# Hybrid GDN block, opening rewritten: x turned before it is normalised, scaled by features on GpSimd; two column operations per block on ScalarE; the second half of x loaded already turned

## The chip, the cores and the metric

The kernel runs on one core of one Trainium2 chip. The metric is the device time of one execution in microseconds (us), the median of the runs. A profiled execution has its own time, and a span, which is the time from the first to the last recorded instruction.

## The reference

One residual block over x (1024 tokens by 1024 features, float32). Six rows of modulation come from a vector c; what the opening of the kernel computes is the first norm, its modulation and the projection of it:

```python
mod = (c_act @ w_ada[l] + b_ada[l])[:, None, :]
shift1, scale1, gate1, shift2, scale2, gate2 = jnp.split(mod, 6, axis=-1)
h = rms_norm(x, norm1_w[l]) * (1.0 + scale1) + shift1
x = x + gate1 * hybrid_mixer(h, w_in[l], ...)      # p = h @ w_in, then gated DeltaNet and a short conv
h = rms_norm(x, norm2_w[l]) * (1.0 + scale2) + shift2
x = x + gate2 * swiglu(h, w_gate[l], w_up[l], w_down[l])
return rms_norm(x, norm_f_w)
```

The norm divides each token (a row of x) by the root of its mean square, so its factor (called rs) belongs to a token; scale1 and shift1 belong to a feature.

## The kernel before, in words

The 1024 tokens are worked in two halves of 512. The 1024 features are eight blocks of 128 (k = 0 to 7). A matmul needs h by features: block k of h is a tile of 128 features by 512 tokens. Every float32 operand of the large products is split into a rounded part and a rest (both in the fast type fp32r, `h[:, 0]` and `h[:, 1]`, or `u[:, 0]` and `u[:, 1]`), and three products are added: high by high, low by high, high by low. TensorE is called PE below, VectorE DVE, ScalarE ACT, GpSimd POOL and SyncE SP.

The program has three orders. The first instructions, up to the accumulators `accs`, are written out by hand and kept in that order on each engine by `seq`. What follows, up to the second norm, is a set of tasks (`load0`, `sums0`, `xh0`, `wsplit0`, `acc0`, `h1_load`, `h1_work`, `fill`, and others). A planner (`Sim`) gives each operation a duration from `cost`, keeps a clock per engine that starts at `T_START`, and picks the next operation by time and the task's priority (`PR`); what it picks is the fixed order of each engine's queue. The rest is written by hand again. Every engine takes its queue strictly in order.

The opening, first half of the tokens:

- SP loads c, then four tiles of x of 128 tokens by 1024 features (`x0`), and then for each k 1 MB of `w_mod` (`wa`, the columns of scale1 and of shift1, turned) and 384 KB of `w_in0` (`wr`).
- `heat_up(n)` puts n matmuls of 128x128 on PE that compute nothing. `HEAT` holds how many at each place; in the trace each is two records. Two large matmuls (`c_ps`) spread silu(c) over the partitions, and DVE copies them into `c_bc`.
- For each tile of x, ACT takes the sum of squares (`norm_rs`), POOL turns it into rs (an add and a power), and DVE (tiles 0 and 1) or ACT (tiles 2 and 3) multiplies the tile by rs.
- `sums0`: for each k, DVE multiplies `wa` by `c_bc` and sums, twice; a small DVE operation after each makes the column `s1c[k]` (the factor of the feature) and `b1c[k]` (its offset).
- `xh0`: for each k, PE turns four 128x128 pieces of the scaled x into a PSUM bank (`tr`); `h_make` has ACT compute `h[:, 0]` and `hf` as tr times s1c plus b1c, and DVE subtract the two for the rest, `h[:, 1]`.
- `wsplit0`: for each k, ACT rounds `wr` into `whl[:, 0]` and DVE subtracts for `whl[:, 1]`.
- `acc0`: for each k, 18 matmuls (three products into six accumulators).

The second half of the tokens: `h1_load` loads four more tiles of x, computes rs for each and multiplies the tile by it on DVE; `h1_work` turns and modulates them in the same way as `xh0`, between the matmuls of `fill`, which multiplies all other columns of `w_in` (loaded as `raw`, split into `u`) by h into banks called `acc`.

Of the kernel before, what the change touches and what calls it, by code (L numbers as in the profile page):

```python
# [13 lines left out]
ALU = mybir.AluOpType  # L14
# [4 lines left out]
HEAT = (16, 2, 20)  # L19
# [15 lines left out]
T_START = (8.7, 10.2, 13.1, 11.7, 2.9)  # L35
# [16 lines left out]
def kernel(  # L52
    ctx: ExitStack,
    tc: tile.TileContext,
    x: bass.AP,
    c_cols: bass.AP,
# [170 lines left out]
    x0 = [xp.tile([P, D], F32, name=nm("x"), tag="x", bufs=8) for _ in range(4)]  # L227
# [18 lines left out]
    heat_up(HEAT[1])  # L246
# [7 lines left out]
    def norm_rs(t, pool, tag, jt="junk"):  # L254
# [4 lines left out]
        rs = pool.tile([P, 1], F32, name=nm("rs"), tag=tag + "r", bufs=4)  # L259
# [8 lines left out]
    late = []  # L268
    for i, t in enumerate(x0):
# [8 lines left out]
        if i == 1:  # L278
# [25 lines left out]
    class Sim:  # L304
# [68 lines left out]
        def cost(self, eng, op, a, k):  # L373
# [29 lines left out]
            elif eng == "pool":  # L403
                busy = 1.1 if op == "tensor_tensor" else 0.5
# [147 lines left out]
    for t, at in [(x0[0], 8.6), (x0[1], 10.0), (x0[2], 11.6), (x0[3], 13.1)] + [(cols_a, 5.0), (nb1, 10.2), (c_act, 4.0), (c_bc, 9.0)]:  # L552
# [7 lines left out]
    chb.take((3, 4, 5))  # L560
# [47 lines left out]

    def sums0():
        cb = c_bc.rearrange("p a b c -> p (a b c)")  # L610
        for k in range(KB):
            sim.wait(lambda: ("wa", k) in done)
# [11 lines left out]

    def xh0():
# [11 lines left out]
    def h_make(k, h, ps, first=None):  # L637
# [9 lines left out]
        free(ps)  # L647
# [3 lines left out]
    def wsplit0():  # L651
        for k in range(KB):
            sim.wait(lambda: k in wr)
# [3 lines left out]
            DVE.tensor_tensor(u[:, 1, :], wr[k], u[:, 0, :].bitcast(F32), ALU.subtract)  # L657
# [3 lines left out]
    def acc0():  # L661
        for _ in range(HEAT[2]):
# [129 lines left out]
    x1 = []  # L792
# [661 lines left out]
    for f, key in ((load0, "load0"), (sums0, "sums0"), (xh0, "h0"), (wsplit0, "w0"), (acc0, "acc")):  # L1454
        sim.spawn(f, PR[key])
# [673 lines left out]
def _laid_out(a):  # L2129
# [4 lines left out]
    d = {n: a[n] for n in ("x", "w_ada", "b_ada", "A_log", "dt_bias", "w_out", "w_gate", "w_up", "w_down", "norm_f_w")}  # L2134
    d["c_cols"] = col(a["c"])
# [10 lines left out]
_ARGS = ["x", "c_cols", "cols", "w_ada", "w_mod", "b_ada", "w_in0", "w_in", "w_ab", "A_log", "dt_bias", "w_out",  # L2146
# [37 lines left out]
```

## Time and profile before

| what | value |
|---|---|
| median of 3 runs | 1170.09 us (1170.09 to 1170.49) |
| profiled execution, its own time | 1170.96 us |
| span of the profiled execution | 1169.1 us |
| PE busy, matmul records | 1159.0 us (99%), 5586 |
| DVE, ACT, POOL busy | 922.0 us (79%), 539.5 us (46%), 61.2 us (5%) |
| mean granted TensorE clock | 0.999 |

In the rows of a timeline the first number is the start in us from the span's start, the second how long it lasted; then the engine (PEld is the weight load that goes ahead of each matmul), the line, the operation, what is written and read by the program's names, the shape, how many instructions were merged into the row (x12), and in brackets how long the engine had been idle and what released it. An instruction of DVE or ACT may start up to 0.1 us before the one ahead of it has ended, so how long a queue needs is read from start to start. Matmuls are pipelined and their ends are modelled, so PE too is read from start to start, on PEld.

### The profile page before, as it was taken

To read this page: it belongs to the slowest core of one execution; us is meant where nothing else is said; L and a number is where in the kernel's file an instruction comes from. 1 tells how busy PE (TensorE), PEld (TensorE's weight loads), DVE (VectorE), ACT (ScalarE), POOL (GpSimd) and SP (SyncE) were. 2 spreads that over 40 slices of the span, in tenths; PEclk is the share of its full clock that TensorE was granted. 3 is DMA by queue.
4 is the path that set the end of the run, shared out by engine and by line. 5 is a ranking of instruction groups with operands and counts; after the bars stand their busy time and mean duration, and the time that the engine had idled before them with its cause. 6 is when DMAs were issued, how large, how long until landed. Compare 5 with 4: busy or idle time off the path is not lost.

```text
span 1169.1 us, 16455 instructions
## 1 busy us (share of the span) xinstructions
PE 1159.0 (99%) x5586; PEld 969.4 (83%) x5586; DVE 922.0 (79%) x1718; ACT 539.5 (46%) x1168; POOL 61.2 (5%) x100
## 2 busy tenths in 40 slices
PE   9999999999999999999999999999999999999997
PEld 7888888888888988888888888888888888888886
DVE  7998988899977998668776777776777687788676
ACT  5688733469633643325433333333333365443343
POOL 2110101002000002100000000000000000000002
PEclk9999999999999999999999999999999999999999
DMA  9624365535215554434264456446554589869413
GB/s 360 257 64 146 106 186 158 174 116 161 81 57 163 164 187 153 194 97 139 95 214 151 149 199 225 151 139 221 192 182 135 197 303 391 310 203 339 146 36 144
DMA packets 126452, 207.06 MB, mean 177 GB/s; under 512 B 20512, under 2 KB 45088, under 8 KB 126368
## 3 DMA queue, kind: packets, MB, share of 16 engines
q1 hardware_dynamic: 120992, 202.80, 51.3%
q10 hardware_dynamic: 5376, 3.21, 0.9%
q8 instruction: 44, 0.72, 0.3%
q14 instruction: 40, 0.33, 0.1%
HBM read 150.91 MB, written 55.05 MB: 176 GB/s over the span
## 4 chain that ended last, share of the span: by engine, by line
PE 92%; DVE 4%; DMA 2%; ACT 1%; issue 1%; SPq 0%; POOL 0%; DVEq 0%; ACTq 0%; POOLq 0%
PE acc L88 34%; PE acc L450 24%; PE dn L88 17%; PE o L450 4%; PE o L88 4%; PE A L450 1%; PE K L450 1%; DVE xo L89 1%; PE ab L450 1%; PE tr L450 1%; PE w L450 1%; PE u L450 1%; PE qk L450 1%; PE kk L450 1%; DMA R<-in_w_gate_dram 1%
## 5 line engine op out<-in xcount | busy, mean ns | idle before, releaser
L450 PE MATMUL acc<-h,u 128*128 128x512 f32 x1200 | 300.2, 398 | 0.0
L450 PEld LDWEIGHTS acc<-h,u 128*128 128x128 f32 x1200 | 219.2, 188 | 41.6
L88 PE MATMUL acc<-h,hl 128*128 128x512 f32 x600 | 140.1, 390 | 0.0
L88 PEld LDWEIGHTS acc<-h,hl 128*128 128x128 f32 x600 | 112.4, 188 | 23.2
L88 PE MATMUL acc<-h,u 128*128 128x512 f32 x456 | 106.1, 389 | 0.0
L88 PE MATMUL acc<-T,hl 128*128 128x512 f32 x432 | 101.4, 390 | 0.1
L88 PEld LDWEIGHTS acc<-h,u 128*128 128x128 f32 x456 | 85.6, 188 | 17.8
L88 PEld LDWEIGHTS acc<-T,hl 128*128 128x128 f32 x432 | 80.9, 188 | 17.2 <-ACT cc L89 0.5
L88 PE MATMUL dn<-h,h 128*128 128x512 f32 x396 | 90.7, 389 | 0.0
L89 DVE TENSOR_TENSOR xo<-xo,dn 128x512 f32<-128x512 f32 x84 | 57.2, 686 | 42.0 <-PE dn L88 34.6
L89 ACT COPY cc<-acc 128x512 f32<-128x512 f32 x66 | 38.4, 590 | 108.3 <-PE acc L88 108.3
L88 PEld LDWEIGHTS dn<-h,h 128*128 128x128 f32 x396 | 74.3, 188 | 15.4
L88 PE MATMUL acc<-T,u 128*128 128x512 f32 x360 | 84.0, 389 | 0.0
L88 PEld LDWEIGHTS acc<-T,u 128*128 128x128 f32 x360 | 67.6, 188 | 14.0
L89 DVE TENSOR_TENSOR cc<-cc,acc 128x512 f32<-128x512 f32 x66 | 43.9, 684 | 29.8 <-PE acc L88 29.8
L450 DVE TENSOR_TENSOR u<-raw,u 128x512 fp32r<-128x512 f32 x82 | 56.3, 688 | 12.2 <-ACT u L450 12.0
L89 DVE TENSOR_TENSOR hl<-R,hl 128x512 fp32r<-128x512 f32 x60 | 39.5, 689 | 33.5 <-ACT hl L89 33.4
L450 ACT CAST u<-raw 128x512 fp32r<-128x512 f32 x61 | 37.8, 621 | 57.8 <-PE acc L450 52.9
L450 DVE SCALAR_TENSOR_TENSOR cv<-pr,cols_a,cv 128x512 f32<-128x512 f32 x72 | 53.2, 747 | 0.3 <-ACT cv L450 0.2
L89 ACT CAST h<-rw 128x512 fp32r<-128x512 f32 x57 | 32.7, 618 | 40.9 <-PE dn L88 34.6
L89 DVE TENSOR_TENSOR u<-R,u 128x512 fp32r<-128x512 f32 x46 | 30.1, 688 | 20.5 <-ACT u L89 20.5
L89 ACT CAST hl<-R 128x512 fp32r<-128x512 f32 x60 | 35.5, 622 | 23.1 <-DVE R L89 10.7
(339 smaller groups left out, 2002.0 us busy)
## 6 DMA issues: line engine op xcount, KB each, us to landing
raw<-in_w_in_dram SPq DMA_DIRECT2D x82, 256.0 KB, 3.1
am_scr<-cc SPq DMA_DIRECT2D x77, 256.0 KB, 4.5
raw<-in_w_ada_dram SPq DMA_DIRECT2D x56, 256.0 KB, 3.2
rw<-am_scr SPq DMA_DIRECT2D x55, 256.0 KB, 5.1
rw<-bm_scr SPq DMA_DIRECT2D x53, 256.0 KB, 5.3
bm_scr<-raw SPq DMA_DIRECT2D x51, 256.0 KB, 5.4
R<-in_w_gate_dram SPq DMA_DIRECT2D x22, 512.0 KB, 3.9
R<-in_w_up_dram SPq DMA_DIRECT2D x22, 512.0 KB, 5.3
```

The costliest lines, as they stand in the source:

```text
L88: return call(*a, **k)
L89: ins = call(*a, **k)
L450: ins = call(*a, **k)
```

## The change

The opening turns x as it comes, without its factor. PE transposes features 128 to 1023 of each tile (`xt`, seven pieces), and DVE (tiles 0 to 2) or ACT (tile 3) copies them into two new tiles `xT` of four feature blocks by 512 tokens. POOL writes a diagonal matrix of each tile's rs (`dgs`). A matmul of ones with it gives rs along the free axis, the same in every partition (`rs_ps`, copied to `RS0` by ACT), and a matmul of x's first 128 features with it gives block 0 turned and scaled at once (`x0_ps`). POOL then multiplies blocks 1 to 7 of `xT` by `RS0` (`x_last`), and `xh0` modulates them from there; the transpositions between the matmuls of `acc0` are gone. The two small operations after each sum are given to ACT. `HEAT` and the planner's start times are new, and three tasks get a priority that rises with k.

For the second half, the host lays x's second 512 tokens out by features as well (`x_t`), `h1_load` loads both layouts (the first only for the squares), spreads rs by one matmul into `RS`, and `h1_work` makes h from `x_t` with two DVE operations and one ACT operation per block and no transposition.

```diff
-HEAT = (16, 2, 20)
+HEAT = (6, 4, 6, 10, 6)
-T_START = (8.7, 10.2, 13.1, 11.7, 2.9)
+W_POOL = ()
+T_START = (11.9, 10.7, 10.0, 11.4, 2.9)
...
-    heat_up(HEAT[1])
...
-    def xnorm(t, pool):
-        rs = norm_rs(t, pool, "n1")[0]
-        DVE.tensor_scalar(t, t, rs, None, ALU.mult)
+    xT = [xp.tile([P, 4, HT], F32, name=nm("xT"), tag="xT", bufs=2) for _ in range(2)]
...
+    def x_part(i, b):
+        lo = 1 if b == 0 else 0
+        return xT[b][:, lo:4, i * P:(i + 1) * P], v3(xt_ps[i, b], 4)[:, lo:4, :]
+
+    heat_up(HEAT[1])
+    dgs = raw_t([P, 4, P])
     for i, t in enumerate(x0):
         rs, sq, p0, p1 = norm_rs(t, sp, "n1")
         seq("act", sq)
         seq("pool", p0)
         seq("pool", p1)
-        if i < 2:
-            seq("dve", DVE.tensor_scalar(t, t, rs, None, ALU.mult))
-        else:
-            late.append((t, rs))
+        seq("pool", POOL.tensor_scalar(dgs[:, i, :], ident, rs, None, ALU.mult))
+        for b in range(2):
+            ps = xt_ps[i, b] = xtb.get("xt")
+            for k in range(4 * b, 4 * b + 4):
+                if k:
+                    seq("pe", PE.transpose(ps[:, (k - 4 * b) * P:(k - 4 * b + 1) * P], t[:, k * P:(k + 1) * P], ident))
+            if i < 3:
+                seq("dve", DVE.tensor_copy(*x_part(i, b)))
+        heat_up(HEAT[2] if i < 3 else HEAT[3])
...
-    for t, rs in late:
-        seq("act", ACT.activation(t, t, AF.Copy, scale=rs))
+    x0_ps, rs_ps = misc.get(), misc.get()
+    for i, t in enumerate(x0):
+        seq("pe", PE.matmul(x0_ps[:, i * P:(i + 1) * P], t[:, 0:P], dgs[:, i, :], start=True, stop=True))
+        seq("pe", PE.matmul(rs_ps[:, i * P:(i + 1) * P], ones, dgs[:, i, :], start=True, stop=True))
...
                 if s_:
-                    DVE.scalar_tensor_tensor(s1c[:, k:k + 1], r, n1c[:, k:k + 1], nb1[:, k:k + 1], ALU.mult, ALU.add)
+                    ACT.activation(s1c[:, k:k + 1], r, AF.Identity, bias=nb1[:, k:k + 1], scale=n1c[:, k:k + 1])
                 else:
-                    DVE.tensor_tensor(b1c[:, k:k + 1], r, bac[:, k:k + 1], ALU.add)
+                    ACT.activation(b1c[:, k:k + 1], r, AF.Identity, bias=bac[:, k:k + 1])
...
+    def x_last():
+        for b in range(2):
+            ecopy(*x_part(3, b))
+        ecopy(RS0, rs_ps)
+        free(rs_ps)
+        for k in range(1, KB):
+            xk = xT[k // 4][:, k % 4]
+            POOL.tensor_tensor(xk, xk, RS0, ALU.mult)
+            done.add(("xn", k))
...
     def xh0():
         for k in range(KB):
-            ps = bank(chb, "tr")
-            for i in range(4):
-                tr(ps[:, i * P:(i + 1) * P], x0[i][:, k * P:(k + 1) * P])
-            sim.wait(lambda: ("cols", k) in done)
+            sim.wait(lambda: ("cols", k) in done and (k == 0 or ("xn", k) in done))
             h = h_slot(k, 0)
-            h_make(k, h, ps, h_hi)
+            h_make(k, h, xT[k // 4][:, k % 4] if k else x0_ps, h_hi)
...
     def acc0():
-        for _ in range(HEAT[2]):
+        for _ in range(HEAT[4]):
             mm(heat[:, 0:P], ones, ident)
...
     def h1_load():
         sim.wait(lambda: "loads0" in done)
-        for tt in range(4, 8):
-            x1.append(load_x(tt, xp, "x", 8))
-        for t in x1:
-            xnorm(t, sp)
+        for i in range(4):
+            t = load_x(4 + i, xp, "x", 4)
+            norm_rs(t, sp, "n1", rs=rs1[:, i:i + 1])
+        for j in range(2):
+            sim.wait(lambda: H[4 * j + 3][0] is not None)
+            t = xp.tile([P, 4, HT], F32, name=nm("xt"), tag="xT", bufs=2)
+            dma(t, x_t[4 * j:4 * j + 4].rearrange("k p c -> p k c"))
+            x1t.append(t)
+        dg = raw((P, 4, P))
+        DVE.tensor_tensor(dg, bc1(ident, 4), bc2(rs1, P), ALU.mult)
+        ps = bank(chb, "RS")
+        mm(ps, ones, flat(dg))
+        free(dg)
+        ecopy(RS, ps)
...
     def h1_work():
-            ps = bank(chb, "tr")
-            for i in range(4):
-                tr(ps[:, i * P:(i + 1) * P], x1[i][:, k * P:(k + 1) * P])
             h = h_slot(k, 1)
-            h_make(k, h, ps)
+            hf = hfs.tile(sp, [P, HT], F32, "hf")
+            DVE.scalar_tensor_tensor(hf, x1t[k // 4][:, k % 4], s1c[:, k:k + 1], RS, ALU.mult, ALU.mult)
+            ACT.activation(h[:, 0, :], hf, AF.Identity, bias=b1c[:, k:k + 1])
+            DVE.scalar_tensor_tensor(h[:, 1, :], hf, b1c[:, k:k + 1], h[:, 0, :].bitcast(F32), ALU.add, ALU.subtract)
```

In the rows of an instruction order that follow, a row is one instruction (or several alike, x3) with its line, operation, what it writes and reads, and the shape written. A name ends in the buffer's number: `x_100` to `x_103` are the four tiles of x, `ps_238` is x0_ps and `ps_239` rs_ps, `raw_138` is dgs, `xt_219` and `xt_223` are the two banks of tile 3.

The queue of PE from its first instruction to the first real matmul, before:

```order
L88 MATMUL heat<-ident,ones 128x128 x16
L88 MATMUL ps_130<-raw_128,ones 128x512
L88 MATMUL ps_134<-raw_132,ones 128x512
L88 MATMUL heat<-ident,ones 128x128 x2
L450 MATMUL heat<-ident,ones 128x128 x3
L450 MATMUL tr_192<-ident,x_100 128x128
L450 MATMUL heat<-ident,ones 128x128 x6
L450 MATMUL tr_192<-ident,x_101 128x128
L450 MATMUL heat<-ident,ones 128x128 x6
L450 MATMUL tr_192<-ident,x_102 128x128
L450 MATMUL heat<-ident,ones 128x128 x5
L450 MATMUL tr_192<-ident,x_103 128x128
```

The queue of PE in the same place, with the change, from the third tile of x on (ahead of these rows stand 6 heats, the two `c_ps`, 4 heats, and for each of the first two tiles 7 transpositions and 6 heats; behind them the two matmuls for each of the other three tiles and 6 more heats):

```order
L90 MATMUL xt_195<-ident,x_102 128x128 x3
L90 MATMUL xt_200<-ident,x_102 128x128 x4
L90 MATMUL heat<-ident,ones 128x128 x6
L90 MATMUL xt_219<-ident,x_103 128x128 x3
L90 MATMUL xt_223<-ident,x_103 128x128 x4
L90 MATMUL heat<-ident,ones 128x128 x10
L90 MATMUL ps_238<-raw_138,x_100 128x128
L90 MATMUL ps_239<-raw_138,ones 128x128
```

Twenty-eight transpositions, eight small matmuls and a different number of heats now stand ahead of the first real matmul, and the four transpositions of each block no longer stand among the real ones.

The queue of ACT between the squares of x's last tile and the first block of h, before:

```order
L89 ACTIVATE x_102<-x_102,rs_163 128x1024
L89 ACTIVATE x_103<-x_103,rs_169 128x1024
L450 CAST whl_198<-wr_195 128x768
L450 ACTIVATE h_0_37_240<-tr_192,b1c,s1c 128x512
L450 ACTIVATE hf_241<-tr_192,b1c,s1c 128x512
```

The same place of ACT with the change:

```order
L463 COPY xT_132<-xt_219 128x3x128
L463 COPY xT_133<-xt_223 128x4x128
L463 COPY RS_266<-ps_239 128x512
L463 ACTIVATE s1c<-mods,nb_130,cols_a 128x1
L463 CAST whl_275<-wr_272 128x768
L463 ACTIVATE b1c<-mods,cols_a 128x1
L463 ACTIVATE h_0_49_303<-ps_238,b1c,s1c 128x512
```

The copy of rs_ps, which needs PE's last small matmul, now stands ahead of the first block's columns, of its weight cast and of h.

The queue of DVE over one block of the opening, before:

```order
L450 TENSOR_TENSOR whl_244<-wr_201,whl_244 128x768
L450 TENSOR_TENSOR b1c<-mods,cols_a 128x1
L450 SCALAR_TENSOR_TENSOR wa_203,mods<-wa_203,c_bc 128x1024
L450 SCALAR_TENSOR_TENSOR s1c<-mods,cols_a,nb_142 128x1
L450 TENSOR_TENSOR h_0_44_278<-hf_279,h_0_44_278 128x512
L450 SCALAR_TENSOR_TENSOR wa_203,mods<-wa_203,c_bc 128x1024
```

DVE with the change, from the end of the hand-written part into the third block:

```order
L463 SCALAR_TENSOR_TENSOR wa_269,mods<-wa_269,c_bc 128x1024 x2
L463 TENSOR_TENSOR whl_275<-wr_272,whl_275 128x768
L463 SCALAR_TENSOR_TENSOR wa_274,mods<-wa_274,c_bc 128x1024
L463 TENSOR_TENSOR h_0_49_303<-hf_304,h_0_49_303 128x512
L463 SCALAR_TENSOR_TENSOR wa_274,mods<-wa_274,c_bc 128x1024
L463 TENSOR_TENSOR whl_307<-wr_278,whl_307 128x768
L463 SCALAR_TENSOR_TENSOR wa_280,mods<-wa_280,c_bc 128x1024
L463 TENSOR_TENSOR h_0_55_337<-hf_338,h_0_55_337 128x512
L463 SCALAR_TENSOR_TENSOR wa_280,mods<-wa_280,c_bc 128x1024
```

The two small operations per block have left DVE; what stays, two sums and two subtractions per block, reads two tiles each.

POOL with the change, from the last tile's rs on; before, its queue went from the power of tile 3 straight to the add of the second half:

```order
L91 TENSOR_SCALAR st_213<-st_213 128x1
L91 TENSOR_TENSOR rs_216<-st_213,nhalf 128x1
L91 TENSOR_SCALAR raw_138<-ident,rs_216 128x128
L463 TENSOR_TENSOR xT_132<-xT_132,RS_266 128x512 x3
L463 TENSOR_TENSOR xT_133<-xT_133,RS_266 128x512 x4
L463 TENSOR_SCALAR st_477<-st_477 128x1
```

Seven multiplications of 128x512 stand on POOL one behind the other, with nothing between them, where it had no work before.

More of the change, by code (lines that the diff above doesn't have):

```diff
@@ L55 @@
     x: bass.AP,
+    x_t: bass.AP,
     c_cols: bass.AP,
@@ L226 @@
     seq("sp", SP.dma_start(out=c_raw, in_=c_cols))
-    x0 = [xp.tile([P, D], F32, name=nm("x"), tag="x", bufs=8) for _ in range(4)]
+    x0 = [xp.tile([P, D], F32, name=nm("x"), tag="x", bufs=4) for _ in range(4)]
     for tt in range(4):
@@ L403, in cost @@
             elif eng == "pool":
-                busy = 1.1 if op == "tensor_tensor" else 0.5
+                busy = (1.1 if n < 128 else 0.1 + n * 0.0026) if op == "tensor_tensor" else 0.5
                 lat = busy + 0.15
@@ L551 @@
     sim.pipe = PIPE0
-    for t, at in [(x0[0], 8.6), (x0[1], 10.0), (x0[2], 11.6), (x0[3], 13.1)] + [(cols_a, 5.0), (nb1, 10.2), (c_act, 4.0), (c_bc, 9.0)]:
+    for t, at in [(t, 10.6) for t in xT] + [(xt_ps[3, 0], 10.0), (xt_ps[3, 1], 10.3), (x0_ps, 11.9), (rs_ps, 12.0), (cols_a, 5.0), (nb1, 9.7), (c_act, 4.0), (c_bc, 7.2)]:
         sim.acc[t.tensor.name] = [[0, P, 0, 1 << 30, at, True, None]]
@@ L559 @@
     dense.take((0, 1, 2))
-    chb.take((3, 4, 5))
+    chb.take((3, 4, 5, 6, 7))
     GP = {t: sim.res(t, 4) for t in ("at", "L", "WQ", "egl", "kt", "Tt", "bk", "nq", "bv")}
@@ L623, in sums0 @@
         done.add("ada0")
+    RS0 = sp.tile([P, HT], F32, name="RS0", tag="RS")
+    def x_last():
[7 more added lines that the diff above has]
+            done.add(("xn", k))
     def xh0():
         for k in range(KB):
[L627 to L630 removed]
+            at_k["h0"] = k
+            sim.wait(lambda: ("cols", k) in done and (k == 0 or ("xn", k) in done))
             h = h_slot(k, 0)
[L632 removed]
+            h_make(k, h, xT[k // 4][:, k % 4] if k else x0_ps, h_hi)
+            if not k:
+                free(x0_ps)
             H[k][0] = h
@@ L656, in wsplit0 @@
             w_hi[k] = u
-            DVE.tensor_tensor(u[:, 1, :], wr[k], u[:, 0, :].bitcast(F32), ALU.subtract)
+            (POOL if k in W_POOL else DVE).tensor_tensor(u[:, 1, :], wr[k], u[:, 0, :].bitcast(F32), ALU.subtract)
             free(wr[k])
@@ L1453 @@
     sim.spawn(h1_load, PR["h1"])
-    for f, key in ((load0, "load0"), (sums0, "sums0"), (xh0, "h0"), (wsplit0, "w0"), (acc0, "acc")):
-        sim.spawn(f, PR[key])
+    for f, key in ((load0, "load0"), (x_last, "setup"), (sums0, "sums0"), (xh0, "h0"), (wsplit0, "w0"), (acc0, "acc")):
+        sim.spawn(f, (lambda n=key: 0.3 + 0.01 * at_k[n] + PR[n] / 1000) if key in at_k else PR[key])
+    sim.own(x0_ps, chb, 6)
+    sim.own(rs_ps, chb, 7)
     for m in heads01:
```

22 lines of the change are left out of this document (15 added, 7 removed).

## The prediction

> **What bounds the kernel now.** The profile's page comes first: how busy each engine is, and the chain of work that ended last.
>
> ```profile
> PE 1159.0 (99%) x5586; PEld 969.4 (83%) x5586; DVE 922.0 (79%) x1718; ACT 539.5 (46%) x1168; POOL 61.2 (5%) x100
> PE 92%; DVE 4%; DMA 2%; ACT 1%; issue 1%; SPq 0%; POOL 0%; DVEq 0%; ACTq 0%; POOLq 0%
> ```
>
> PE is both the busiest engine and the chain. The waits of PE over the whole span have five groups; the two that the change can reach are
>
> ```profile
> PE acc L450 <- ACT h L450: 0.9, 1, 0.9
> PE tr L450 <- DVE x L89: 0.3, 1, 0.3
> ```
>
> So from the first real matmul on PE hardly ever waits. The time is then: when that matmul starts, plus all work queued on PE behind it, plus any wait that a change adds. I read each from the timeline of the opening, PE and its weight loads first:
>
> ```profile
> 1.44 5.33 PEld L88 LDWEIGHTS heat<-ident,ones 128*128 128x128 f32 x25 [1.44 <-POOL ident masks.py:199]
> 8.02 0.19 PEld L88 LDWEIGHTS ps<-raw,ones 128*128 128x128 f32 x1 [0.24 <-issue]
> 8.45 0.19 PEld L88 LDWEIGHTS ps<-raw,ones 128*128 128x128 f32 x1 [0.24 <-issue]
> 12.41 1.42 PEld L450 LDWEIGHTS heat<-ident,ones 128*128 128x128 f32 x12
> 13.75 0.14 PEld L450 LDWEIGHTS tr<-ident,x 128*128 128x128 f32 x1
> 13.86 1.20 PEld L450 LDWEIGHTS heat<-ident,ones 128*128 128x128 f32 x10
> 15.09 0.27 PE L450 MATMUL tr<-ident,x 128*128 128x128 f32 x1
> 15.40 0.78 ACT L450 ACTIVATE h<-tr,b1c,s1c 128x512 fp32r<-128x512 f32 x1 [1.53 <-PE tr L450]
> 16.23 0.96 PE L450 MATMUL acc<-h,whl 128*128 128x512 f32 x3 [0.87 <-ACT h L450]
> 25.40 0.60 PEld L450 LDWEIGHTS tr<-ident,x 128*128 128x128 f32 x4
> 25.97 4.05 PEld L450 LDWEIGHTS acc<-h,whl 128*128 128x128 f32 x18
> 30.06 0.59 PEld L450 LDWEIGHTS tr<-ident,x 128*128 128x128 f32 x4
> 52.88 3.63 PEld L450 LDWEIGHTS ab<-h,wab 128*128 128x128 f32 x16
> ```
>
> From these: warm, the 12 records of 6 heats take 13.75 − 12.41 = 1.34 us, 0.223 per heat; a transposition takes 13.86 − 13.75 = 0.11; a record of a large float32 matmul 8.45 − 8.02 = 0.43, two to a matmul. The first 25 heat records take about 0.213 each, twice the later rate, until about 6.7 us. One block of acc0 takes 30.06 − 25.97 = 4.09 for its 18 matmuls, and its four transpositions 25.97 − 25.40 = 0.57. The last transposition ended at 15.36, ACT began h at 15.40, and PE began 0.83 after that: 16.23. The eight blocks ended at 52.88.
>
> **Part 1, PE's queue ahead of the first matmul.** Now 6 heats at half speed, 12 × 0.213 = 2.56, end at 4.00. The two c_ps have four records, 0.85 each at half speed, 0.43 later; with the clock rising at 6.7 as before they end at 7.0. Then 4 heats, 28 transpositions, 28 heats and 8 small float32 matmuls of two records each (a heat's price): 0.89 + 3.1 + 6.25 + 1.8 = 12.0. PE queues these back to back, since x's tiles and rs come earlier: the last power on POOL ended at 11.94 before, and dgs adds one small operation.
>
> ```profile
> 10.97 0.97 POOL L89 TENSOR_TENSOR rs<-st,nhalf 128x1 f32<-128x1 f32 x1
> ```
>
> So rs_ps is there at 19.05 and a little, some 19.3. ACT's queue stands behind it, in the order shown: the copy of RS0, s1c, the weight cast, b1c, h. Their steps from start to start:
>
> ```profile
> 54.90 0.59 ACT L450 COPY pr<-acc 128x512 f32<-128x512 f32 x1 [1.64 <-DVE cv L450]
> 55.39 0.64 ACT L450 ACTIVATE qkT<-cv 128x512 f32<-128x512 f32 x1
> 44.93 0.84 ACT L450 CAST whl<-wr 128x768 fp32r<-128x768 f32 x1 [1.25 <-issue]
> 45.67 0.78 ACT L450 ACTIVATE h<-tr,b1c,s1c 128x512 fp32r<-128x512 f32 x1
> 2.57 0.21 ACT L89 ACTIVATE c_act<-raw 128x8 f32<-128x8 f32 x1
> ```
>
> Copy 0.5, cast 0.74, the two column operations 0.1 to 0.2 each (a tiny activation is 0.21 long): h begins at about 20.95, PE at 21.8, which is **+5.55** against 16.23. The six heats behind the small matmuls end before that. The clock's rise can shift this by about 0.9 either way.
>
> **Part 2, transpositions off PE's stream.** Seven groups stood between the blocks and eight in the second half: 15 × 0.56 = **−8.4**. The new matmul of RS has two records of 0.43: **+0.86**. Without any wait, parts 1 and 2 give −2.0.
>
> **Part 3, two column operations per block to ACT.** DVE's block before:
>
> ```profile
> 23.11 0.95 DVE L450 TENSOR_TENSOR whl<-wr,whl 128x768 fp32r<-128x768 f32 x1
> 23.98 0.15 DVE L450 TENSOR_TENSOR b1c<-mods,cols_a 128x1 f32<-128x1 f32 x1
> 24.05 1.22 DVE L450 SCALAR_TENSOR_TENSOR wa<-wa,c_bc 128x1024 f32<-128x1024 f32 x1
> 25.32 0.22 DVE L450 SCALAR_TENSOR_TENSOR s1c<-mods,cols_a,nb 128x1 f32<-128x1 f32 x1
> 25.72 0.69 DVE L450 TENSOR_TENSOR h<-hf,h 128x512 fp32r<-128x512 f32 x1 [0.18 <-ACT hf L450]
> 26.33 1.22 DVE L450 SCALAR_TENSOR_TENSOR wa<-wa,c_bc 128x1024 f32<-128x1024 f32 x1
> 27.47 0.95 DVE L450 TENSOR_TENSOR whl<-wr,whl 128x768 fp32r<-128x768 f32 x1
> ```
>
> 27.47 − 23.11 = 4.36 per block, under PE's 4.66. Without b1c and s1c and their waits it is 0.87 + 1.14 + 0.61 + 1.14 = 3.76, under PE's new 4.1 by only 0.34. So this part is worth nothing by itself and keeps DVE just ahead. ACT, with 0.4 more per block, has room. The loads are behind nothing new: their buffers (five of wa, three of wr) are freed by DVE, and they can run that many blocks ahead of it.
>
> **Part 4, seven multiplications on POOL.** The trace has none of 128x512. What it does have is POOL and DVE at once:
>
> ```profile
> 64.91 1.85 POOL L450 MEMSET xbd<- 128x1024 f32 x2 [4.15 <-DVE x L450]
> 66.02 0.76 DVE L450 TENSOR_SCALAR raw<-raw 128x16 f32<-128x16 f32 x1
> 376.25 1.63 POOL L450 COPY A<-xbd 32x256 f32<-32x256 f32 x3
> 376.80 0.83 DVE L450 TENSOR_TENSOR u<-raw,u 128x512 fp32r<-128x512 f32 x1 [1.53 <-ACT u L450]
> L450 DVE TENSOR_TENSOR u<-raw,u 128x512 fp32r<-128x512 f32 x82 | 56.3, 688 | 12.2 <-ACT u L450 12.0
> L450 POOL COPY A<-xbd 32x256 f32<-32x256 f32 x8 | 3.6, 455 | 7.8 <-DMA xbd<-dx 7.6
> ```
>
> DVE's tiny operation at 66.02 took 0.76 us and ended at 66.78, when POOL's second fill ended (64.91 + 1.85 = 66.76): held for the whole of POOL's instruction. The subtraction at 376.80 took 0.83 instead of the mean 0.688 beside POOL's copies. All four DVE operations of a block have that form, two tiles read from SBUF. So I expect POOL and DVE to take turns. [...]
>
> POOL's price p: its copy of 256 elements averages 0.455, so 512 elements with one input are about 0.8 to 0.9, and two inputs read in turn at most 1.8; below, DVE's own 0.69 is the least I allow. I take 1.2, nearer the copy's row. [...]
>
> Place: POOL begins when RS0 is copied, at 20.0. DVE waits for the first weight cast until 20.8, so one product is mostly covered. From then on they alternate until POOL is through: 7p + (0.87 + 1.14 + 0.61 + 1.14) × 2 = 7p + 7.52 after 20.0 the columns of block 2 are ready; column, h and the step to PE add 1.1. PE could have begun block 2 at 21.8 + 8.2 = 30.0. The loss is 7p − 1.4: **+7.0** for p = 1.2, 4.2 for 0.8, 11.2 for 1.8. After block 2 DVE needs 3.76 against 4.1 and PE does not wait again; the slack is too thin to give anything back, for PE cannot make up time. If POOL got in only where DVE idles, each block would pay about p less 0.34: 7 × 1.2 − 6 × 0.34 − 0.9 = 5.5.
>
> **Part 5, the second half.** DVE now does 16 operations of about 0.67 where it did 8 subtractions, four scalings of x and four of hf; some 1 us more, and 2 MB more are loaded. Both are spread over 40 us in which the matmuls of fill do not need h yet; I cost them at nothing. If that cover were gone, PE would wait about 1 to 3 us.
>
> **Sum.** 5.55 − 8.4 + 0.86 + 7.0 = +5.0. Against the profiled execution's own 1170.96 (span 1169.1) that is 1176.0; that execution lies 0.9 above the median of the runs, so I say 1175.1.
>
> **Rivals.**
>
> *POOL does not hold DVE.* For: a subtraction beside POOL lost only 0.14. Against: the row at 66.02. It would give −2.0, 1168.1. The point from which it decides: with p replaced by what DVE really loses per product, 7p − 1.4 is under 2.0 below 0.49 us, and the kernel is then not slower. Chance 0.22.
>
> *The heats cost less than their records.* If PE were through with its queue as soon as rs allows (12.2 + 1.8), RS0's copy starts at 14.3, h at 15.9, PE at 16.7 instead of 21.8: 5.1 less, 1170.0 with POOL's turns. For: the ends of matmuls are modelled, and nothing waits for a heat's result. Against: 0.223 per heat, measured with nothing else on PE. Chance 0.07.
>
> *PE's clock falls in the new waits.* PE would wait two or three times for about 2 us between 24 and 37 us. The first rows show heats at half speed until about 5 us of work had gone by; one such fall would cost 2.5 us or more: 1178 to 1181. Against: PE's longest wait in this trace after its start is the 0.9 us quoted above, so nothing shows a fall. [...] Chance 0.10.
>
> **How the numbers follow.** A measurement of this kernel can tell about 0.2%, 2.3 us. The forecast, 0.61, runs from 1172 to 1179 with p from 0.8 to 1.6 and the clock's 0.9, nearly all of it slower. The first rival lies 2.0 below, so split: 0.09 faster, 0.13 same; the second 0.06 and 0.01 for its two ends; the third slower. With 0.04 of the forecast within 0.2%: faster 0.15, same 0.18, slower 0.67. The range takes in the first rival below and most of the third above: 1167 to 1180.
>
> **What would show it.** Right: the first acc matmul near 21.8, after ACT's copy of RS0 near 19.3; POOL's products 1.0 to 1.6 us each, back to back or in turn with DVE; DVE's sums between 21 and 36 us starting late or lasting 1 us more than 1.22; PE waiting for ACT h in blocks 0 to 2 for some 7 us in all, and not afterwards; ab beginning near 61.7 instead of 52.88. Wrong: a first acc matmul before 18; DVE's steps at 3.8 per block beside POOL; a wait of PE after 65 us.

## The result: 0.5% slower, and the profile after

The changed kernel takes 1176.47 us (median, 1176.12 to 1177.55) beside 1170.34 us for the kernel before on the same chip: a ratio of 1.0049, with a 95% interval of 1.0039 to 1.006. The forecast was 1175.1 us, with a chance of 0.67 for slower by over 0.2%.

The busy times and the chain of the changed kernel's page:

```profile
PE 1161.2 (99%) x5580; PEld 969.6 (83%) x5580; DVE 925.1 (79%) x1702; ACT 541.7 (46%) x1186; POOL 72.9 (6%) x111
PE 90%; DVE 5%; ACT 3%; issue 1%; DMA 1%; POOL 0%; DVEq 0%; ACTq 0%; POOLq 0%
```

PE's share is 99% as before, and POOL, with 11.7 us more, goes from 5% to 6% and stays at 0% of the chain. Shares hide the loss. The waits of PE over the whole span (us in all, times, longest) show where to look:

```profile
PE acc L463 <- ACT h L463: 3.9, 3, 1.8
PE acc L463 <- DVE h L463: 1.0, 1, 1.0
```

Before, PE waited 0.9 us for h in all. The timeline of the opening has the cause (start, duration, engine, operation):

```profile
18.43 0.30 PEld L90 LDWEIGHTS ps<-raw,ones 128*128 128x128 f32 x2
18.96 0.58 ACT L463 COPY RS<-ps 128x512 f32<-128x512 f32 x1 [3.43 <-PE ps L90]
19.63 13.54 POOL L463 TENSOR_TENSOR xT<-xT,RS 128x512 f32<-128x512 f32 x7 [6.87 <-ACT RS L463]
20.78 0.78 ACT L463 ACTIVATE h<-ps,b1c,s1c 128x512 fp32r<-128x512 f32 x1
21.61 3.04 PE L463 MATMUL acc<-h,whl 128*128 128x512 f32 x12 [1.35 <-ACT h L463]
21.63 2.31 DVE L463 SCALAR_TENSOR_TENSOR wa<-wa,c_bc 128x1024 f32<-128x1024 f32 x1
23.88 1.76 DVE L463 TENSOR_TENSOR h<-hf,h 128x512 fp32r<-128x512 f32 x1
25.68 1.22 PEld L463 LDWEIGHTS acc<-h,whl 128*128 128x128 f32 x6 [1.46 <-DVE h L463]
27.79 2.01 DVE L463 TENSOR_TENSOR whl<-wr,whl 128x768 fp32r<-128x768 f32 x1
29.15 4.18 PEld L463 LDWEIGHTS acc<-h,whl 128*128 128x128 f32 x12 [2.25 <-ACT h L463]
...
33.64 1.21 DVE L463 SCALAR_TENSOR_TENSOR wa<-wa,c_bc 128x1024 f32<-128x1024 f32 x1
33.77 1.22 PEld L463 LDWEIGHTS acc<-h,whl 128*128 128x128 f32 x6 [0.44 <-DVE h L463]
34.78 0.95 DVE L463 TENSOR_TENSOR whl<-wr,whl 128x768 fp32r<-128x768 f32 x1
57.41 1.13 PEld L463 LDWEIGHTS ab<-h,wab 128*128 128x128 f32 x5
62.31 2.48 PEld L463 LDWEIGHTS ab<-h,wab 128*128 128x128 f32 x11
```

Three things are to be read here. PE's first real matmul starts at 21.61, 5.38 later than before. While POOL's seven products run, 19.63 to 33.17, every DVE operation but the first, six in all, lasts 1.06 to 1.10 us longer than later: a sum 2.31 instead of 1.21, the rest of whl 2.01 instead of 0.95, the rest of h 1.76 instead of the 0.69 of before. (The first, the rest of whl at 20.58, lasts 0.17 longer.) And five of ab's matmuls now stand inside acc0. Counted without them, acc0 ends at 62.31 − 1.13 = 61.18, where it ended at 52.88.

That moment splits the difference in two. Up to the end of acc0 the change loses 61.18 − 52.88 = 8.30 us; from there on it gains, since 1169.1 − 52.88 = 1116.2 us were left before and 1174.7 − 61.18 = 1113.5 now: 2.7. Together they are 5.6, the difference of the two spans. The same split is used for every experiment below ("up to acc0's end" and "rest"): acc0's end is the start of ab's last row less the time of ab's rows ahead of it.

### The profile page after: what moved, and what is told of

Same layout as the page of the kernel before. It is cut to its first block, busy times and chain, and to the rows that moved or that the text cites. A ratio compares the mean times of both kernels' runs of the same rounds, so it can differ in the third digit from the quotient of the medians.

```text
span 1174.7 us, 16452 instructions
## 1 busy us (share of the span) xinstructions
PE 1161.2 (99%) x5580; PEld 969.6 (83%) x5580; DVE 925.1 (79%) x1702; ACT 541.7 (46%) x1186; POOL 72.9 (6%) x111
## 4 chain that ended last, share of the span: by engine, by line
PE 90%; DVE 5%; ACT 3%; issue 1%; DMA 1%; POOL 0%; DVEq 0%; ACTq 0%; POOLq 0%
PE acc L90 35%; PE acc L463 22%; PE dn L90 17%; PE o L90 4%; PE o L463 4%; PE A L463 1%; PE heat L90 1%; PE K L463 1%; DMA raw<-in_w_ada_dram 1%; PE ab L463 1%; DVE xo L91 1%; DVE cv L463 1%; DVE u L463 1%; DVE T L91 1%; PE kk L463 0%
## 5 line engine op out<-in xcount | busy, mean ns | idle before, releaser
L463 ACT CAST u<-raw 128x512 fp32r<-128x512 f32 x65 | 40.2, 620 | 47.0 <-PE acc L463 44.7
```

The lines of the kernel that those rows point to most:

```text
L463: ins = call(*a, **k)
```

## The experiments

Ratios are to the kernel before, run alternately with each on the same chip, with 95% intervals; the changed kernel's is 1.0049. One per cent is 11.7 us.

| what | ratio | first acc | acc0's end | rest |
|---|---|---|---|---|
| before | 1 | 16.23 | 52.88 | 1116.2 |
| changed kernel | 1.0049 (1.0039 to 1.006) | 21.61 | 61.18 | 1113.5 |
| no products | 0.9995 (0.9986 to 1.0004) | 21.37 | 54.77 | 1113.2 |
| fills instead | 0.9995 (0.9986 to 1.0004) | 21.05 | 54.45 | 1113.8 |
| one-input products | 1.0003 (0.9994 to 1.0013) | 22.04 | 56.91 | 1114.2 |
| no heats | 1.0009 (1.0 to 1.0019) | 18.25 | 57.81 | 1112.4 |
| second half as before | 1.008 (1.0066 to 1.0094) | 22.38 | 62.12 | 1117.8 |
| second half alone | 1.0061 (1.0044 to 1.0078) | 16.21 | 59.78 | 1120.1 |
| columns on DVE | 1.0172 (1.0156 to 1.0187) | 21.41 | 64.56 | 1126.8 |
| columns on DVE, other order | 1.0067 (1.0053 to 1.008) | 21.82 | 65.15 | 1111.8 |
| changed, other order | 1.0128 (1.0114 to 1.0141) | 21.95 | 61.51 | 1125.2 |
| all turned by diag(rs) | 1.0037 (1.0023 to 1.005) | 16.89 | 51.35 | 1123.8 |
| the same, second order | 0.9975 (0.9966 to 0.9984) | 16.94 | 51.10 | 1117.2 |
| the same, third order | 0.9947 (0.9934 to 0.9961) | 17.17 | 51.05 | 1113.4 |

### Do POOL's products hold DVE?

```diff
-            POOL.tensor_tensor(xk, xk, RS0, ALU.mult)
```

> The changed kernel without GpSimd's seven multiplications of the turned x by RS; this leaves the factor rs out of blocks 1 to 7 of the first half. Turns theory (the 6.75 us that acc0 loses between its first matmul and its end come from VectorE and GpSimd taking turns): the loss goes, VectorE's sums last 1.22 us again from the start, TensorE still starts near 21.6, and the time is 1176.5 - 6.75 = about 1169.7 us. Rival (GpSimd does not hold VectorE; TensorE waits because the late start pushes ScalarE's and VectorE's work of the first blocks together): the waits of blocks 0 to 2 stay and the time stays at 1176 to 1177.

Measured: 0.9995, that is 0.54% or 6.3 us less than the changed kernel. The timeline of the opening without products, and its rows of ab:

```profile
21.22 1.22 DVE L463 SCALAR_TENSOR_TENSOR wa<-wa,c_bc 128x1024 f32<-128x1024 f32 x1
...
24.99 1.22 DVE L463 SCALAR_TENSOR_TENSOR wa<-wa,c_bc 128x1024 f32<-128x1024 f32 x1
28.75 1.22 DVE L463 SCALAR_TENSOR_TENSOR wa<-wa,c_bc 128x1024 f32<-128x1024 f32 x1
...
50.99 1.10 PEld L463 LDWEIGHTS ab<-h,wab 128*128 128x128 f32 x5
55.87 2.52 PEld L463 LDWEIGHTS ab<-h,wab 128*128 128x128 f32 x11
```

TensorE starts as late as in the changed kernel, but DVE's sums last 1.22 us from the first on, its block takes 28.75 − 24.99 = 3.76 us, and acc0 ends at 54.77, 6.4 earlier. PE then waits for nothing between its first acc and acc0's end. The late start alone doesn't make the waits. The turns do.

### Is it POOL's reading or POOL's being busy?

Two kernels put another POOL instruction in the same place, seven times, on RS's own tile.

```diff
-            POOL.tensor_tensor(xk, xk, RS0, ALU.mult)
+            POOL.memset(RS0, 0.0)                                # the first kernel
+            POOL.tensor_scalar(RS0, RS0, 1.0, None, ALU.mult)    # the second
```

> The changed kernel with each of GpSimd's seven multiplications replaced by a fill of RS's own 128x512 tile: GpSimd writes as much as before and reads nothing; this leaves the factor rs out of blocks 1 to 7 of the first half. If what holds VectorE is GpSimd's reading, its sums stay at 1.22 us beside the fills and the time is that of the kernel without products, 6 us under the changed kernel: a ratio to before of about 0.9995, 1169.7 us. If any GpSimd instruction takes its turn (a 128x1024 fill was 0.93 us in the trace of before, so half a microsecond for this one), seven turns cost about 3.5 - 1.4 = 2 us: 1171.8 us. If the length of the instruction does not matter, 1176.

> The changed kernel with each of GpSimd's seven multiplications replaced by a multiplication of RS's own 128x512 tile by 1.0: one input from SBUF in place of two; this leaves the factor rs out of blocks 1 to 7 of the first half. Theory (any GpSimd instruction that reads SBUF takes its turn, for as long as it lasts): a copy of 256 elements on 32 partitions was 0.455 us, so about 0.9 us each, a loss of 7 x 0.9 - 1.4 = 4.9 instead of 6.75: 1174.6 us, VectorE's sums 0.8 us longer than 1.22. Rival (only a GpSimd instruction with two inputs holds VectorE): like the run with fills, 1169.7 us, a ratio of 0.9995.

Measured: 0.9995 with fills, 1.0003 with one input. The timeline with fills, then with one input:

```profile
19.05 4.02 POOL L463 MEMSET RS<- 128x512 f32 x7 [6.11 <-ACT RS L463]
20.90 1.22 DVE L463 SCALAR_TENSOR_TENSOR wa<-wa,c_bc 128x1024 f32<-128x1024 f32 x1
```

```profile
20.06 13.98 POOL L463 TENSOR_SCALAR RS<-RS 128x512 f32<-128x512 f32 x7 [6.63 <-ACT RS L463]
21.89 1.63 DVE L463 SCALAR_TENSOR_TENSOR wa<-wa,c_bc 128x1024 f32<-128x1024 f32 x1
24.48 1.21 DVE L463 SCALAR_TENSOR_TENSOR wa<-wa,c_bc 128x1024 f32<-128x1024 f32 x1
25.63 1.35 DVE L463 TENSOR_TENSOR whl<-wr,whl 128x768 fp32r<-128x768 f32 x1
28.05 1.08 DVE L463 TENSOR_TENSOR h<-hf,h 128x512 fp32r<-128x512 f32 x1
```

Three operations of DVE fall beside the fills, and they last 0.96, 1.22 and 0.69 us, as without them: POOL's writing costs DVE nothing here. With one input POOL still needs 2.0 us per instruction from start to start, which fits waiting for DVE; but DVE loses only some 0.40 at a time, on each rest of whl or h (1.35 beside 0.95, 1.08 beside 0.69) and on the first sum (1.63), and nothing on the other sums. Against the run without products that is 56.91 − 54.77 − (22.04 − 21.37) = 1.5 us at acc0's end, or 0.9 in the median (the intervals overlap). Neither theory named this: it is a turn, but a shorter one, and why it spares the later sums is open. In these runs what held DVE was a POOL instruction that reads: 1.06 to 1.10 us at a time beside the products of two tiles, some 0.40 with one input, nothing beside the fills.

### Is the late start PE's own queue?

```diff
-HEAT = (6, 4, 6, 10, 6)
+HEAT = (6, 4, 0, 0, 0)
```

> The changed kernel with the 22 heats between the four transposed tiles and the 6 after RS left out (HEAT = (6, 4, 0, 0, 0)); nothing that is computed changes. Queue theory (the late start is TensorE's own queue ahead of RS): RS comes some 5.3 us earlier, TensorE starts near 16.3 instead of 21.6, and the time is 1176.5 - 5.3 = about 1171.2 us. Rival 1 (the start is set by the loads, the sums of squares and ScalarE's chain to rs): it starts no more than 2 us earlier, 1174.5 to 1176.5. Rival 2 (without heats the granted clock falls behind the gaps): transpositions and the first matmuls at half speed, 1176.5 or more.

The edit takes 28 heats out ahead of RS (three times six, and ten), not 22.

Measured: 1.0009, 4.7 us less than the changed kernel, near the 5.3 of the queue theory, but not by its way. PE starts at 18.25, not 16.3: the start gained 3.4, acc0's end 3.4 too, and 1.1 more of the span came later and is not assigned. The timeline shows what held the start:

```profile
12.03 1.21 DVE L463 SCALAR_TENSOR_TENSOR wa<-wa,c_bc 128x1024 f32<-128x1024 f32 x1
12.43 2.36 POOL L91 TENSOR_SCALAR raw<-ident,rs 128x128 f32<-128x128 f32 x1
13.17 1.21 DVE L463 SCALAR_TENSOR_TENSOR wa<-wa,c_bc 128x1024 f32<-128x1024 f32 x1
14.85 0.30 PEld L90 LDWEIGHTS ps<-raw,x 128*128 128x128 f32 x2 [2.27 <-POOL raw L91]
18.25 7.11 PE L463 MATMUL acc<-h,whl 128*128 128x512 f32 x18 [2.69 <-ACT h L463]
```

The last diag(rs), 0.62 to 0.64 us long for the other tiles, lasted 2.36. It started beside a sum of DVE and ended at 14.79, just behind the second sum (13.17 + 1.21 = 14.38). That fits the same turns with the roles changed, in this one case: DVE was first and POOL waited, and PE waited for POOL.

The rival on the clock was right in part. Behind idle weight loads of 2.27 and 2.88 us the first 18 matmuls took 7.11 us, beside 4.46 for a block in the trace of before, and the mean granted clock of the run was 0.996, beside 0.999. It doesn't show in the time: PE waited for h of block 1 behind them all the same (0.85 us), and block 1 began 3.4 us earlier than in the changed kernel, by as much as block 0 did.

### What are the transpositions of the second half worth?

One kernel takes the changed opening with the old second half, the other the old opening with the new second half.

```diff
-            t = load_x(4 + i, xp, "x", 4)              # changed kernel: also xT tiles, RS, no tr
+            x1.append(load_x(tt, xp, "x", 4))          # x by tokens, scaled on VectorE
...
+            ps = bank(chb, "tr")
+            for i in range(4):
+                tr(ps[:, i * P:(i + 1) * P], x1[i][:, k * P:(k + 1) * P])
```

> The changed kernel with the second half as it was: x by tokens, scaled on VectorE, eight groups of four transpositions, no RS matmul; the opening is the changed one. Theory (a group is worth its 0.56 us of TensorE wherever it stands): 1176.5 + 4.5 - 0.9 = about 1180 us, all of it after 61 us. Rival (the transpositions fill gaps, so the part by features brings nothing): 1176.5. Rival (the plan of the work that follows falls out otherwise, as in the kernel with the second half alone): a wait of several microseconds at a place that the edit does not touch.

Measured: 1.008, that is 0.31% or 3.6 us more than the changed kernel, as the theory had it. The size is in part luck: behind acc0 its PE has 2.3 us of small waits (K 1.0, A 0.9, G 0.4) that the changed kernel hasn't. In its timeline the transpositions stand in rows such as this one, 0.15 us each, between 76.4 and 88.5 us:

```profile
80.09 0.60 PEld L463 LDWEIGHTS tr<-ident,x 128*128 128x128 f32 x4
```

```diff
-    x0 = [xp.tile([P, D], F32, name=nm("x"), tag="x", bufs=8) for _ in range(4)]
+    x0 = [xp.tile([P, D], F32, name=nm("x"), tag="x", bufs=4) for _ in range(4)]
```

> The kernel before with the second half's part of the change alone: x of the second half loaded by features, no transpositions there, RS by one matmul; the opening is the old one. Theory (each group of four transpositions that leaves TensorE's queue is worth its 0.56 us, eight of them are 4.5, RS costs 0.86): 1170.3 - 3.6 = about 1166.7 us. Rival 1 (the transpositions lay in gaps of TensorE or VectorE's extra sum per block comes into the bound): 1170 to 1172. Rival 2 (loading x twice delays the second half's start by a wait): over 1172.

Measured: 1.0061, 11 us off the theory, and on the side of its second rival. This kernel doesn't test the transpositions, and the trace says why. Its longest wait of PE, and its timeline:

```profile
PE acc L452 <- ACT h L452: 5.5, 2, 4.6
```

```profile
43.73 0.49 PE L452 MATMUL tr<-ident,x 128*128 128x128 f32 x3
43.92 0.33 SPq L452 DMA_DIRECT2D x<-in_x_dram  x1
47.49 1.06 ACT L452 ACTIVATE jk<-x 128x1024 bf16<-128x1024 f32 x1 [5.13 <-DMA x<-in_x_dram]
52.65 0.76 ACT L452 ACTIVATE h<-tr,b1c,s1c 128x512 fp32r<-128x512 f32 x1
53.46 1.22 PE L452 MATMUL acc<-h,whl 128*128 128x512 f32 x2 [4.59 <-ACT h L452]
```

The tiles for the turned layout left room for four x tiles only, and the old opening reads its four until block 7 is turned (43.73). So the second half's first load is issued at 43.92, ACT's sum of squares stands in its queue waiting for it, and block 7's h stands behind that. acc0 ends 6.9 later. The new second half needs the new opening, which is through with x's tiles when its last small matmul has read them, at 18.7. The rest is 3.9 longer than before, too, where 3.6 less was expected; PE waits there for raw (1.9 us) and for A (1.6), in another order of the later work. How much of them the turned loads cause was not separated.

### Are the columns better on DVE?

```diff
-                    ACT.activation(s1c[:, k:k + 1], r, AF.Identity, bias=nb1[:, k:k + 1], scale=n1c[:, k:k + 1])
+                    DVE.scalar_tensor_tensor(s1c[:, k:k + 1], r, n1c[:, k:k + 1], nb1[:, k:k + 1], ALU.mult, ALU.add)
-                    ACT.activation(b1c[:, k:k + 1], r, AF.Identity, bias=bac[:, k:k + 1])
+                    DVE.tensor_tensor(b1c[:, k:k + 1], r, bac[:, k:k + 1], ALU.add)
...
-BIAS = dict(dve=0.3)     # the second kernel only
+BIAS = dict(dve=0.45)
```

> The changed kernel with its two column operations per block (s1c and b1c of the first half) back on VectorE. Turns theory: VectorE's block grows by two column operations, about 0.6 us, in the stretch in which GpSimd holds it back (blocks 0 to 2, some 2 us) and is about as long as TensorE's 4.1 afterwards: 1177.5 to 1179.5 us. Rival (the columns on ScalarE hold up h and cause part of TensorE's waits for ScalarE): 1 to 3 us faster than the changed kernel, 1173.5 to 1175.5.

> The changed kernel with the column operations of the first half back on VectorE, as in the run before of that kind, with one number of the planner changed (BIAS of VectorE 0.3 to 0.45) so that the order of the later work comes out anew. In the earlier run the stretch of 20 to 40 us lost 3.8 us more than in the changed kernel, and 10 us more were lost between 400 and 510 us. Theory (only the first is the price of the two operations): 1176.5 + 3.8 = about 1180 us, a ratio of 1.008. Rival (the columns on VectorE really cost 15 us): about 1191.

Measured: 1.0172 and 1.0067. The first is 12 us over the top of its forecast, nearly all of it in the rest; the second is near its 1.008. Up to acc0's end both lose about the same against the changed kernel, 3.4 and 4.0 us, where about 2 was expected at first. In the timeline of the second:

```profile
26.36 1.24 DVE L463 SCALAR_TENSOR_TENSOR s1c<-mods,cols_a,nb 128x1 f32<-128x1 f32 x1
30.60 1.21 DVE L463 TENSOR_TENSOR b1c<-mods,cols_a 128x1 f32<-128x1 f32 x1
31.73 1.21 DVE L463 SCALAR_TENSOR_TENSOR wa<-wa,c_bc 128x1024 f32<-128x1024 f32 x1
31.90 0.81 ACT L463 ACTIVATE h<-xT,b1c,s1c 128x512 fp32r<-128x512 f32 x1 [8.75 <-DVE b1c L463]
32.77 7.22 PEld L463 LDWEIGHTS acc<-h,whl 128*128 128x128 f32 x21 [5.04 <-ACT h L463]
36.65 0.15 DVE L463 TENSOR_TENSOR b1c<-mods,cols_a 128x1 f32<-128x1 f32 x1
```

An operation on one column, 0.15 us at 36.65, lasts 1.21 beside a product: it can pay a whole turn, however small. But the sum right behind it (31.73) pays none. The seven products hold DVE for 6.7 us in all, here as in the changed kernel: the price was the same with nine DVE operations beside the products as with seven there. What the columns cost is their place in the queue. Block 1's b1c now stands behind s1c and the rest of whl, which in the changed kernel are not ahead of it, so ACT's h starts at 31.90 instead of 28.29, PE waits 5.04 us for it, and block 1 begins at 32.77, where the changed kernel begins it at 29.15. That is 3.6 of the 4.0 us. Moving the two columns to ACT is worth that much beside the products; without products it was not tried. The first kernel's rest is 13.3 longer than the changed kernel's. About half of that is one wait of PE, for the split of the last gate's sum:

```profile
PE row L90 <- ACT Tt L463: 6.8, 1, 6.8
```

That wait is gone in the second kernel, whose later order was dealt anew by one number of the planner; its rest is even 1.7 shorter than the changed kernel's.

### A version without the products

If the loss is turns and a late start, both can go: turn and scale every block, not only block 0, by a matmul with diag(rs).

```diff
-                    seq("pe", PE.transpose(ps[:, (k - 4 * b) * P:(k - 4 * b + 1) * P], t[:, k * P:(k + 1) * P], ident))
+                seq("pe", PE.matmul(to, t[:, k * P:(k + 1) * P], dgs[:, i, :], start=True, stop=True))
...
-        ecopy(RS0, rs_ps)
-            POOL.tensor_tensor(xk, xk, RS0, ALU.mult)
```

> A version meant to beat both: the second half as in the changed kernel; in the first half all eight blocks, not only block 0, are turned and scaled in one matmul against diag(rs), so RS0, GpSimd's products and all heats after the first ten go, and the turned blocks are copied out of PSUM by VectorE (tiles 0 and 1) and by the planned copies (tiles 2 and 3). The small matmuls wait for diag(rs) of each tile. Theory: no turns, TensorE starts near 16.3 to 18.3 (GpSimd's last diag(rs) waited 2 us for VectorE in the run without heats), and the rest is the changed kernel's: 1176.5 - 6.75 - 3.3 to 5.3 = 1164.5 to 1166.5 us. Rival (the clock of TensorE stays low without the heats, or VectorE's copies hold up its sums): 1168 or more.

Measured: 1.0037, not the gain. The opening does what it should: the first acc at 16.89, acc0's end at 51.35, 9.8 before the changed kernel. The rest is 10 us longer. Its longest wait of PE, and the windows behind it (us, busy time of PE, PEld, DVE, ACT and POOL with counts, granted clock, DMA share, GB/s):

```profile
PE row L90 <- ACT Tt L460: 6.7, 1, 6.7
```

```profile
482.00:486.00 4.00, 3.65 (x8) 2.64 (x9) 1.00 (x2) 4.00 (x8) 1.43 (x5) 0.50 1.01 409
486.00:490.00 4.00, 4.00 (x14) 3.16 (x13) 1.37 (x2) 0.46 (x2) 1.67 (x4) 0.67 0.81 325
```

PE waits 6.7 us, then runs at half its clock (0.50), and still at 0.67 in the four microseconds after that. A new opening makes the planner deal out another order 400 us later, and in this order PE reaches the last gate's matmul before its sum is ready.

Two more orders of the same kernel, each by numbers of the planner alone:

```diff
-MARGIN = dict(pe=0.6)
+MARGIN = dict(pe=0.7)                            # second order
-BIAS = dict(dve=0.3)                             # third order, with MARGIN 0.7
+BIAS = dict(dve=0.25)
-T_START = (14.9, 11.6, 10.0, 12.8, 2.9)
+T_START = (14.2, 11.0, 10.0, 12.8, 2.9)
```

> The version with all eight blocks turned and scaled by diag(rs), with one number of the planner changed (MARGIN 0.6 to 0.7), so that it writes the order after 65 us out anew; in the first version TensorE waited 6.7 us at 475 us for the split of the last gate's sum, which stood too early in its queue, and ran at half speed for some us after it, 9 to 10 us in all. Theory (that wait is an accident of the order, not a price of the opening): it goes, and the time is 1175.9 - 9.4 = about 1166.5 us, a ratio of about 0.995. Rival (whatever the order, something the opening saved is paid back later): a wait of similar size elsewhere, 1174 or more.

> The version with all eight blocks turned and scaled by diag(rs), with the planner's numbers set otherwise again (MARGIN 0.7, BIAS of VectorE 0.25, TensorE's and VectorE's start times 14.2 and 11.0 instead of 14.9 and 11.6). The first order of this version gave 1175.9, the second 1168.0 us with some 7 us of small waits left between 20 and 400 us. Theory (the opening is worth about 10 us against the changed kernel, and an order decides how much of it is kept): no wait over 2 us after 65 us, 1164 to 1168 us. Rival (the gain of the second order was a lucky one): 1172 or more.

Measured: 0.9975 (1167.99 us) and 0.9947 (1166.08 us, beside 1171.58 for the kernel before in the same comparison). In the second the wait is gone, but its rest is still 3.8 us longer than the third's, in smaller waits, so the theory's 1166.5 was missed by 1.5. Both orders beat the kernel before and the changed one, the third by 0.5% and 1.0%. Its longest wait of PE, but for the first heat's:

```profile
PE acc L460 <- ACT h L460: 1.5, 1, 1.5
```

Was it the planner's number rather than the opening? The changed kernel with that number alone:

> The changed kernel, nothing edited but the planner's MARGIN, 0.6 to 0.7, as in the second order of the turned and scaled version. It separates the planner's number from the opening. Theory (the number only deals the later order out anew; here the planner's own account puts VectorE's last work 22 us behind TensorE's instead of 9, as in the first order of the turned and scaled version): the opening loses the same 6.75 us, a wait for the split of the last gate's sum of some 7 us comes up near 475 us, 1185 us. Rival (MARGIN 0.7 is the better number for any opening): under 1174.

Measured: 1.0128, 9 us worse than the changed kernel. Up to acc0's end nothing moved (61.51), and the wait came up where it was looked for:

```profile
PE row L90 <- ACT Tt L463: 7.7, 1, 7.7
```

So the number is not better in itself; it deals another order, good for one opening and bad for another. What all three orders of the new opening share is acc0's end, 51.05 to 51.35, some 10 us before the changed kernel's. How much of that reaches the end depends on the order: three were tried for this opening, two for the changed kernel and one for the kernel before, so the 0.5% is the opening together with a chosen order.

## Why the prediction was right, point by point

**Part 1, the late start.** Predicted +5.55, measured +5.38. The last small matmul's weights were loaded by 18.73 where 19.05 was worked out, ACT's steps came in the listed order (copy at 18.96, h at 20.78), and the first acc at 21.61. Two small misses cancel: the copy came 0.3 us earlier than worked out, and the two columns took 0.3 each instead of 0.1 to 0.2. The run without heats shows that the heats are real work in PE's queue, against the second rival; what that rival lacked was that the last diag(rs) would then meet DVE's sums. That the half speed of the first heats is the clock's, no run shows: the granted clock stands at 1.00 from 0 to 10 us in both traces.

**Part 2, the transpositions.** Seven groups before acc0's end are 3.92 by the predicted price. The run without products, where PE waits for nothing in acc0, takes 54.77 − 21.37 = 33.40 us for it beside 52.88 − 16.23 = 36.65 before, so they brought 3.25, or 0.46 a group instead of 0.56. From there on, 3.62 was predicted (eight groups less RS's matmul) and 2.7 measured between the two traces; the run with the second half as before gives 3.6 in the median and 4.3 in its rest, small waits included. The mechanism holds; the price of a group was about 0.1 too high, and 8 × 0.46 − 0.86 = 2.8 would have met the 2.7.

**Part 3, the columns.** DVE's block without them and without turns is 3.76 us in the run without products, the predicted number. That the part is worth nothing by itself no run tests. Beside the products it is worth 3.4 to 4.0 us up to acc0's end, by the place of b1c in DVE's queue, and the prediction had no term for that.

**Part 4, the turns.** Predicted 7p − 1.4 = 7.0 for p = 1.2, the author's estimate: the trace of before has no product of that size. Measured: 8.30 − 5.38 + 3.92 = 6.84 between the traces (6.2 with the 3.25 above), 6.3 in the median when the products go. The hold was 1.06 to 1.10 us per DVE operation; with 1.08 for p the formula gives 6.2, and with the 0.40 of the one-input run 1.4, where 1.5 and 0.9 were measured. The shortest product lasted 1.265 us. The median is 2.0, outside the 1.0 to 1.6 named as a sign, which fits POOL waiting its turn as well:

```profile
L463 POOL TENSOR_TENSOR xT<-xT,RS x7: 1265/2006/2275, 19.6 to 30.9; 128x512 f32<-128x512 f32 x7
```

The row that the turns were first read from is another matter. The prediction took the operation at 66.02 to be held by POOL's fill, and carried that over to operations that read two tiles. In the same stretch of that trace, in the middle of the fills (64.91 to 66.76), a subtraction of just that form is not held:

```profile
65.42 0.68 DVE L450 TENSOR_TENSOR u<-raw,u 128x512 fp32r<-128x512 f32 x1
```

The run with fills says the same. The operation at 66.02 reads one tile; the other five of its kind last 0.11 to 0.17 us, and what held this one no run here separates. So the turns came as forecast, but from that row by luck; the subtraction beside POOL's copies was the better ground.

**Part 5, the second half's extra work,** cost nothing that can be seen: PE waits for none of it.

**The total.** The start, the turns and the second half came out at 5.38, 6.84 and −2.7, where 5.55, 7.0 and −3.62 were forecast; with 3.92 for the seven groups that is 5.6 between the traces against 5.0, and the miss is the second half. Two of the signs looked different. PE's waits for h add up to 4.9 us in the list, not some 7, since part of the loss stands in slow matmuls, as told below. And ab began at 57.41, not near 61.7, because the planner put five of its matmuls into acc0; without them the mark is 61.18.

**The rivals.** That POOL doesn't hold DVE fell with the run without products, and its border (0.49 us lost per product) is where the one-input run sits: 0.40 lost at a time, and no difference from before. The clock did fall in the new waits. The windows of the changed kernel:

```profile
21.60:29.10 7.50, 4.69 (x18) 3.23 (x18) 7.50 (x7) 2.85 (x6) 7.50 (x5) 1.00 0.65 211
29.10:33.70 4.60, 4.55 (x12) 3.34 (x12) 4.60 (x5) 1.82 (x3) 4.07 (x2) 0.63 0.63 199
```

After PE's idle weight loads of 1.46 and 2.25 us, the clock granted from 29.1 to 33.7 was 0.63, and twelve matmuls took 4.18 us. The forecast had given this rival 2.5 us or more, and it cost nothing. The six matmuls behind them waited for DVE's rest of h until 33.77 (0.44 us), which turns had set. From the start of the twelve to the start of the six it was 4.62 us here; in the run with the second half as before, and in the changed kernel's other order, it was 4.61 and 4.60, while the twelve took 3.60 and 3.94.

## What to carry to other kernels

Before giving an elementwise step to GpSimd, look at what VectorE does in that stretch: beside GpSimd products of two SBUF tiles, VectorE, with instructions that read two SBUF operands, paid a turn of 1.06 to 1.10 us for six of seven products, and an instruction on a single column paid one as well (1.21 us instead of 0.15); the price was these turns, 6.7 us in all, where GpSimd's busy share went from 5% to 6%. A step that only scales rows before a transposition can ride in the transposing matmul instead: here acc0 then ended at 51.05 to 51.35, beside 61.18 with the products. And where a planner deals out the order, judge a local change up to a fixed mark in the program and the rest by itself; a bad order 400 us later can cost as much as the edit gained (here a rest 10 us longer against 9.8 us gained).

## What the runs showed of the hardware that was not expected

- The turns seem to go both ways: a 128x128 GpSimd operation of 0.63 us took 2.36 with two VectorE sums in its time (one case).
- Seven GpSimd products of 128x512 held VectorE for 6.7 us in all, whether it had long operations in its queue or single columns between them.
- A GpSimd fill of 128x512 ran seven times in 4.02 us beside VectorE without any effect on it; a GpSimd multiplication with one input took 2.0 us from start to start and held VectorE for 0.40 at a time.
- The clock of TensorE was 0.63 over 4.6 us after two gaps of 1.46 and 2.25 us with six matmuls between them. After one of 6.7 us it was 0.50 over four us of work and 0.67 over the next four.
